# Latent attention: which engine rounds the weights and scales the first blocks' probabilities

## The chip, the cores and the metric

The program runs on one core of one Trainium2 chip. The metric is device time in microseconds (us). Three runs of the kernel before took 751.84, 752.97 and 751.84 us, median 751.84. One further execution was recorded by the hardware profiler; everything that is read from a profile or a trace below is from that one execution.

## The reference

One decoder block on 512 tokens of width 1024, float32. What matters here is the middle of it:

```python
xn = rmsnorm(x, norm_mix_g)
q_lat, kv_lat, k_rope, dq, dk, dv, gate_pre = split(xn @ w_in)
q  = rmsnorm(q_lat)  @ mla_w_uq      # 8 heads, 64 plain + 32 rotary columns each
kv = rmsnorm(kv_lat) @ mla_w_ukv     # 8 heads, 64 key + 64 value columns each
o_mla  = causal_attention([q_nope, rope(q_pe)], [k_nope, rope(k_rope)], v)   # softmax over 512 keys
o_diff = rmsnorm(attn(dq1, dk1, dv) - lam * attn(dq2, dk2, dv))              # 4 heads
x = x + (sigmoid(g1) * (o_mla @ w_branch_mla) + sigmoid(g2) * (o_diff @ w_branch_diff)) @ w_out
x = x + (silu(hn @ w_gate) * (hn @ w_up)) @ w_down
```

## The kernel before

**Products of three.** Every large matrix product is made of three matmuls. Each float32 operand is cut into a rounded high part and the rest, its low part, and `mm3` adds high x high (L301), high x low (L302) and low x high (L303) into one PSUM tile. For weights, `weights` loads a `raw` tile of up to 128x1024 (4 buffers), takes a `w` tile of twice that size (3 buffers), and calls `round_hi` (a copy that rounds: L264 on ScalarE or L266 on VectorE) and `round_lo` (raw minus high part: L269, on VectorE or GpSimd). The list `w_eng` says which engines do the two. The rest of the work that follows a product is the same everywhere: `split` writes a PSUM result as high part (ScalarE, L251 or L253) and low part (VectorE, L255 or L257).

**Stages.** At first the input is transposed and the latents are projected (to about 50 us in the trace). The middle stage holds both attentions and lasts to about 290 us: 8 heads of latent attention in 4 pairs, then 4 heads of differential attention. Then come the branch projections, the output projection and the feed-forward network, which is over half of the time and which the change does not touch.

**What sets the order in the middle stage.** A scheduler orders each engine's instructions by priority. The attention heads are written in `with urgent()`, so they go first whenever they are ready. Between them the scheduler places filling work, listed in `FILL`, `FILL_MLA` and `FILL_DIFF`: `mqk` (queries and keys of a pair of heads), `mv` and `v` (values), `pe` (rotary part of the queries), `mr` (DMAs that copy the rotated parts into the heads' tiles), `qk` (queries and keys of a differential head) and `gate` (gate projections). Each engine then runs its own instructions strictly in the order that the program holds.

**A head of latent attention** (`mla_head`) works through four blocks of queries, of 128, 256, 384 and 512 keys. For each, TensorE makes the scores (L633) in one of two `sc` tiles of PSUM. VectorE adds the mask and finds the maximum (L637), which also empties the `sc` tile. ScalarE takes the exponential with its sum (L156). VectorE inverts the sum (L640), and the block is multiplied by it: the first two blocks on GpSimd (L772, `P_POOL`), the other two on ScalarE (L774). Then TensorE transposes the blocks (L659) and multiplies them with the values (L781). A third block of scores cannot be written before the first one's tile has been emptied by L637.

**GpSimd's other work in the stage** stays: two of the four steps of the rotation of each differential projection (L566 and L567), part of the norm after each differential head (L698, L711), and the low parts of three weight tiles at the start of the stage (a gate and the first pair of latent heads), which are still under `W_ENG0`.

Of the kernel before, what the change touches and what calls it, by code (L numbers as in the profile page):

```python
# [17 lines left out]
ALU = mybir.AluOpType  # L18
# [25 lines left out]
W_POOL = "a0 a1 a4 b0 b1 b2 b3 b4 b5 b6 b7".split()  # L44
W_DVE = "b0 b1 b2 b3 b4 b5 b6 b7".split()
N_WARM = 8
P_POOL = (0, 1)
W_ENG0 = ['act', 'pool']
W_ENG = ['dve', 'pool']
W_ENG_DIFF = ['act', 'dve']  # L50
FILL = [[("gate", 0, 0)], [], [("pe", 0), ("mr", 0), ("gate", 0, 1), ("mv", 0)]]
FILL_MLA = [[("mqk", 1), ("mr", 1), ("v", 0), ("pe", 1)],
            [("mqk", 2), ("mr", 2), ("v", 1), ("mv", 1)],
# [40 lines left out]
def build(ctx, nc, tc, a, out):  # L94
# [12 lines left out]
    def PS(tag):  # L107
        return pp.tile([P, 512], F32, name=nm("ps_" + tag), tag=tag, bufs=PBUFS[tag])
# [151 lines left out]
    w_eng = list(W_ENG0)  # L260
# [219 lines left out]
    def gate(b, m):  # L480
        w = weights(kview("w_in", C_G + b * D + m * P, P), KD, P)
        ps = PS("mm")
        for k in range(KD):
            mm3(ps, [w[s][:, k, :] for s in range(2)], xa(k), k == 0, k == KD - 1)
        if m % 2 == 0:
            gate_tiles[b, m] = LF()
        gates[b, m] = gate_tiles[b, m - m % 2][:, (m % 2) * S:(m % 2 + 1) * S]
        nc.vector.tensor_mul(out=gates[b, m], in0=ps, in1=x_rms)
# [12 lines left out]
    def fill(work):  # L501
        for kind, *args in work:
            if kind == "gate":
                gate(*args)
            elif kind == "v":
                diff_v(*args)
            elif kind == "qk":
                qk[args[0]] = diff_qk(*args)
            elif kind == "pe":
                pe[args[0]] = mla_pe(*args)  # L510
            elif kind == "mv":
                mv[args[0]] = mla_v(*args)
            elif kind == "mqk":
                mqk[args[0]] = mla_qk(*args)
            elif kind == "mr":
                mla_rope(args[0], mqk[args[0]], pe[args[0] // 2])
# [66 lines left out]
    def diff_qk(h):  # L583


        u = diff_project(C_DQ + h * P)
        qs, k = [L_(), L_()], L_()
        for m, own, other in ((0, low, high), (1, high, low)):
            split(u[own], qs[0][own, m, :], qs[1][own, m, :], DIFF_SCALE)
            for q in qs:  # L590
                dma(r32(q[other, m, :]), r32(q[own, m, :]))
        u = diff_project(C_DK + h * P)
        for m, own, other in ((0, low, high), (1, high, low)):
            split(u[own], k[own, m, :], k[other, m, :])
        return [[(q[:, m, :], k[:, m, :]) for q in qs] for m in range(2)]
# [4 lines left out]
    def diff_v(c):  # L600
        w = [weights(kview("w_in", C_DV + c * 256, 256, k0, 4), 4, 256) for k0 in (0, 4)]
        for tp in range(2):
            ps = PS("mm")
            for t in range(2):
                for k in range(KD):
                    mm3(ps[:, t * 256:(t + 1) * 256], xa(k, slice((2 * tp + t) * P, (2 * tp + t + 1) * P)),
                        [w[k // 4][s][:, k % 4, :] for s in range(2)], k == 0, k == KD - 1)
            l = L_()
            for t in range(2):
                cs = slice(t * 256, (t + 1) * 256)  # L610
                split(ps[:, cs], l[:, 0, cs], l[:, 1, cs], x_rs[:, 2 * tp + t:2 * tp + t + 1])
            dv.append(l)


    def rope_key():
        pt = PS("tr")
        for t in range(NB):
            nc.tensor.transpose(out=pt[0:RD, t * P:(t + 1) * P], in_=latn[t][:, 640:672], identity=ident)
        kpe = L_()[0:RD]
        rope(pt[0:RD, :], kpe[:, 0, :], kpe[:, 1, :], cos_m, sin_m, shuf_m, 1.0, RD)  # L620
        return kpe
# [96 lines left out]
    def mla_pe(g):  # L718
        w = weights([a["mla_w_uq"][0][k * P:(k + 1) * P, :].rearrange("p (h d) -> p h d", d=96)
                     [:, 4 * g:4 * g + 4, 64:96] for k in range(3)], 3, P)  # L720
        ps = PS("mm")
        for k in range(3):
            mm3(ps, [w[s][:, k, :] for s in range(2)], [lat[k][:, s, :] for s in range(2)], k == 0, k == 2)
        pe = L_()
        rope(ps, pe[:, 0, :], pe[:, 1, :], cos_m, sin_m, shuf_m, MLA_SCALE)
        return pe
# [23 lines left out]
    def mla_v(g):  # L750
        w = weights(kview("mla_w_ukv", g * 512, 512), 2, 512, [(4, 64, 128)])
        v = []
        for tp in range(2):
            ps = PS("mm")
            for t in range(2):
                for k in range(2):
                    mm3(ps[:, t * 256:(t + 1) * 256],
                        [lat[3 + k][:, s, (2 * tp + t) * P:(2 * tp + t + 1) * P] for s in range(2)],
                        [w[s][:, k, :] for s in range(2)], k == 0, k == 1)
            l = T("L", [P, 2, 4, 2, 64], F32R)  # L760
            pv = ps.rearrange("p (t h d) -> p t h d", t=2, h=4)
            split(pv, l[:, :, :, 0, :], l[:, :, :, 1, :])
            v.append(l)
        return v

    def mla_head(qk, v, pair, o, h):
        q, k = qk[h]
        blocks = []
        for i, p in enumerate(prob_tiles()):
            r, = scores([([(q[0:96, a_, :], k[0:96, b_, :]) for a_, b_ in ((0, 0), (0, 1), (1, 0))], p)], i)  # L770
            if i in P_POOL:
                nc.gpsimd.tensor_scalar(out=p, in0=p, scalar1=r, scalar2=0.0, op0=ALU.mult, op1=ALU.add)  # L772
            else:
                nc.scalar.activation(out=p, in_=p, func=AF.Copy, scale=r)  # L774
            blocks.append(p)
        pt = transposed(blocks)
        c = 2 * (pair % 2) + h
        ps = PS("pv")
        for s in range(2):
            for j in range(NB):  # L780
                nc.tensor.matmul(out=ps[:, j * P:S], lhsT=v[j // 2][:, j % 2, c, :, :].rearrange("p s d -> p (s d)"),  # L781
                                 rhs=pt[:, s, OFF[j]:OFF[j] + S - j * P], start=s == 0 and j == 0,
                                 stop=s == 1 and j == NB - 1)
        u = tmp()[:64]
        nc.scalar.activation(out=u, in_=ps[64:P, :], func=AF.Copy)
        nc.vector.tensor_add(out=u, in0=ps[0:64, :], in1=u)
        rows = slice(64 * h, 64 * h + 64)
        split(u, o[rows, 0, :], o[rows, 1, :])
# [13 lines left out]
    mqk, pe, mv = {}, {}, {}  # L802
    fill([("mqk", 0)])
    kpe = rope_key()
    fill(FILL[2])
    o_mla = []
    for p in range(4):
        o = L_()
        o_mla.append(o)
        w_eng[:] = W_ENG  # L810
        fill(FILL_MLA[p])
        with urgent():
            for h in range(2):
                mla_head(mqk[p], mv[p // 2], p, o, h)


    o_diff, parts = [], []
    w_eng[:] = W_ENG_DIFF
    for h in range(4):
        fill(FILL_DIFF[h])  # L820
        with urgent():
# [179 lines left out]
```

## Time and profile before

| | |
|---|---|
| Three runs, us | 751.84, 752.97, 751.84 |
| The profiled execution's own time, us | 753.9 |
| Its span, us | 752.1 |
| TensorE busy | 737.0 us, 98% of the span |
| VectorE busy | 414.7 us, 55% |
| ScalarE busy | 326.8 us, 43% |
| GpSimd busy | 104.3 us, 14% |

Rows of the profile name the engines PE (TensorE matmuls), PEld (its weight loads), DVE (VectorE), ACT (ScalarE), POOL (GpSimd) and SP (SyncE, which issues the DMAs). L269 is line 269 of the kernel. In a group's row stand the shapes, how often it occurs, its busy time in us, the mean time of one in ns, and the idle time before it with what ended it. A timeline's row begins with its start and its length in us; idle time before it stands in brackets at the end. A matmul's length is modelled, and matmuls overlap in the pipe, so the pace is read from the distance of their starts. PEclk is the share of the TensorE clock that was granted.

### The profile page before, as it was taken

What the parts mean: (1) busy time and instruction counts of PE and PEld (TensorE: products, weight loads), DVE (VectorE), ACT (ScalarE), POOL (GpSimd) and SP (SyncE); (2) the same over time, 40 slices, a digit from 0 to 9 for tenths busy, and PEclk for the clock granted to TensorE, in tenths of its full rate; (3) what the DMA queues carried; (4) which work ended last, traced back from release to release, by engine and by line L of the source; (5) the groups of instructions that cost most, each with busy time, mean ns of one, the idle gap of its engine ahead of it and who ended that gap; (6) DMA issues with size and microseconds to landing.
All of it is one profiled execution on the core that took longest, in us unless ns stands there. A gap on an engine that the chain in (4) does not pass through costs nothing.

```text
span 752.1 us, 9652 instructions
## 1 busy us (share of the span) xinstructions
PE 737.0 (98%) x3639; PEld 623.0 (83%) x3639; DVE 414.7 (55%) x800; ACT 326.8 (43%) x609; POOL 104.3 (14%) x94
## 2 busy tenths in 40 slices
PE   7999999999999999999999999999999999999996
PEld 5988889888888888788898888888888888888885
DVE  6968688898998745595453323333333332122424
ACT  6564558587667535644233323232322223122314
POOL 3505252631341001000000000000000000000302
PEclk9999999999999999999999999999999999999999
DMA  8404333552433322248023333333323232322203
GB/s 300 124 1 117 106 87 96 135 126 69 110 87 87 107 85 85 84 140 278 2 85 108 89 97 99 98 99 87 109 85 111 85 112 85 109 88 92 106 0 113
DMA packets 99820, 76.74 MB, mean 102 GB/s; under 512 B 6303, under 2 KB 86973, under 8 KB 99773
## 3 DMA queue, kind: packets, MB, share of 16 engines
q1 hardware_dynamic: 99773, 76.12, 34.3%
q8 instruction: 29, 0.48, 0.3%
q14 instruction: 18, 0.15, 0.1%
HBM read 69.81 MB, written 2.10 MB: 96 GB/s over the span
## 4 chain that ended last, share of the span: by engine, by line
PE 81%; DVE 9%; ACT 5%; POOL 2%; issue 2%; DMA 1%; SPq 0%; DVEq 0%; ACTq 0%
PE ps_mm L301 22%; PE ps_mm L303 22%; PE ps_mm L302 22%; PE ps_sc L633 2%; PE ps_sc L301 1%; PE ps_sc L302 1%; PE ps_tr L301 1%; PE ps_tr L302 1%; PE ps_tr L303 1%; PE ps_sc L303 1%; POOL t L567 1%; PE ps_tr L659 1%; ACT L L495 1%; DVE w L269 1%; DVE X L355 1%
## 5 line engine op out<-in xcount | busy, mean ns | idle before, releaser
L302 PE MATMUL ps_mm<-X,w 128*128 128x512 f32 (+1 forms) x568 | 217.0, 382 | 0.0
L301 PE MATMUL ps_mm<-X,w 128*128 128x512 f32 (+1 forms) x568 | 216.9, 382 | 0.1
L303 PE MATMUL ps_mm<-X,w 128*128 128x512 f32 (+1 forms) x568 | 216.6, 382 | 0.0
L269 DVE TENSOR_TENSOR w<-raw,w 128x1024 fp32r<-128x1024 f32 x92 | 116.3, 1266 | 165.4 <-ACT w L264 165.2
L264 ACT ACTIVATE w<-raw 128x1024 fp32r<-128x1024 f32 (+1 forms) x98 | 101.1, 1036 | 181.2 <-issue 78.9
L303 PEld LDWEIGHTS ps_mm<-X,w 128*128 128x128 f32 x568 | 106.9, 188 | 19.9 <-POOL w L269 0.3
L301 PEld LDWEIGHTS ps_mm<-X,w 128*128 128x128 f32 x568 | 106.7, 188 | 19.9 <-DVE t L565 0.2
L302 PEld LDWEIGHTS ps_mm<-X,w 128*128 128x128 f32 x568 | 106.8, 188 | 19.7 <-DVE X L255 0.2
L936 POOL TENSOR_TENSOR L<-L,P 128x512 f32<-128x512 f32 (+1 forms) x9 | 11.6, 1299 | 439.0 <-ACT t L935 439.0
L909 ACT ACTIVATE t<-ps_mm 128x512 f32<-128x512 f32 x22 | 13.2, 598 | 80.9 <-PE ps_mm L303 80.9
L910 DVE TENSOR_TENSOR t<-t,ps_mm 128x512 f32<-128x512 f32 x22 | 15.1, 688 | 59.7 <-PE ps_mm L303 59.7
L156 ACT ACTIVATE P<-P,sm 128x128 f32<-128x128 f32 (+3 forms) x64 | 35.8, 560 | 27.4 <-DVE sm L637 27.0
L269 POOL TENSOR_TENSOR w<-raw,w 128x1024 fp32r<-128x1024 f32 (+3 forms) x22 | 37.3, 1701 | 57.5 <-PE ps_tr L472 25.8
L633 PE MATMUL ps_sc<-L,L 96*128 96x128 f32 (+7 forms) x160 | 36.5, 327 | 1.5 <-DVE sm L637 1.5
L302 PE MATMUL ps_mm<-w,L 128*128 128x512 f32 (+1 forms) x100 | 37.2, 372 | 0.0
L301 PE MATMUL ps_mm<-w,L 128*128 128x512 f32 (+1 forms) x100 | 37.2, 374 | 0.0
L303 PE MATMUL ps_mm<-w,L 128*128 128x512 f32 (+1 forms) x100 | 37.1, 373 | 0.0
L301 PE MATMUL ps_mm<-L,w 128*128 128x512 f32 x90 | 35.2, 393 | 0.5 <-ACT w L264 0.5
L302 PE MATMUL ps_mm<-L,w 128*128 128x512 f32 x90 | 35.5, 394 | 0.0
L303 PE MATMUL ps_mm<-L,w 128*128 128x512 f32 x90 | 35.2, 393 | 0.0
L251 ACT ACTIVATE L<-t 64x512 fp32r<-64x512 f32 (+2 forms) x47 | 29.1, 623 | 13.6 <-POOL t L567 6.2
L255 DVE TENSOR_TENSOR L<-t,L 128x512 fp32r<-128x512 f32 (+2 forms) x37 | 29.6, 801 | 4.8 <-ACT L L251 4.5
(265 smaller groups left out, 1231.9 us busy)
## 6 DMA issues: line engine op xcount, KB each, us to landing
raw<-w_in SPq DMA_DIRECT2D x28, 512.0 KB, 4.0
raw<-w_ffn_gate SPq DMA_DIRECT2D x22, 512.0 KB, 3.9
raw<-w_ffn_up SPq DMA_DIRECT2D x22, 512.0 KB, 3.9
raw<-w_ffn_down SPq DMA_DIRECT2D x22, 512.0 KB, 3.6
L<-L SPq DMA_DIRECT2D x32, 128.0 KB, 2.9
raw<-w_out SPq DMA_DIRECT2D x8, 512.0 KB, 3.7
L<-x SPq DMA_DIRECT2D x8, 256.0 KB, 6.1
raw<-w_branch_mla SPq DMA_DIRECT2D x4, 512.0 KB, 3.4
```

The source lines that it names most:

```text
L156: return nc.scalar.activation(**kw)
L251: nc.scalar.activation(out=hi, in_=src, func=AF.Copy, scale=scale)
L255: nc.vector.tensor_sub(out=lo, in0=src, in1=r32(hi))
L264: nc.scalar.activation(out=o, in_=i, func=AF.Copy)
L269: (nc.vector if w_eng[1] == 'dve' else nc.gpsimd).tensor_sub(out=o, in0=i, in1=r32(hi))
L301: nc.tensor.matmul(out=o, lhsT=lh, rhs=rh, start=start, stop=False)
L302: nc.tensor.matmul(out=o, lhsT=lh, rhs=rl, start=False, stop=False)
L303: return nc.tensor.matmul(out=o, lhsT=ll, rhs=rh, start=False, stop=stop)
L633: nc.tensor.matmul(out=ps[:, :n], lhsT=q[:, i * P:n], rhs=k[:, 0:n], start=j == 0, stop=j == last)
L909: last_silu = nc.scalar.activation(out=g, in_=gate_ps, func=AF.Silu)
L910: nc.vector.tensor_mul(out=g, in0=g, in1=ps)
L936: nc.gpsimd.tensor_mul(out=xs, in0=xs, in1=g)
```

## The change

The two low-level helpers stay as they are; only the engines that they use in the latent attention's part change.

- From the filling work that follows `rope_key()` on (`FILL[2]`) and through `FILL_MLA`, high parts of weights are made on ScalarE and low parts on VectorE. Before, `FILL[2]` had ScalarE and GpSimd, and `FILL_MLA` VectorE and GpSimd. The differential part had ScalarE and VectorE already and keeps them.
- The first two blocks' probabilities of each latent head are multiplied on VectorE, not on GpSimd.

```diff
-P_POOL = (0, 1)
+P_DVE = (0, 1)
 W_ENG0 = ['act', 'pool']
-W_ENG = ['dve', 'pool']
-W_ENG_DIFF = ['act', 'dve']
+W_ENG = ['act', 'dve']
@@ mla_head
-            if i in P_POOL:
-                nc.gpsimd.tensor_scalar(out=p, in0=p, scalar1=r, scalar2=0.0, op0=ALU.mult, op1=ALU.add)
+            if i in P_DVE:
+                nc.vector.tensor_scalar(out=p, in0=p, scalar1=r, scalar2=None, op0=ALU.mult)
             else:
                 nc.scalar.activation(out=p, in_=p, func=AF.Copy, scale=r)
@@ the middle stage
     kpe = rope_key()
+    w_eng[:] = W_ENG
     fill(FILL[2])
     o_mla = []
     for p in range(4):
         o = L_()
         o_mla.append(o)
-        w_eng[:] = W_ENG
         fill(FILL_MLA[p])
@@ the differential heads
-    w_eng[:] = W_ENG_DIFF
     for h in range(4):
```

Since the scheduler places everything anew, the order changes on all engines in the middle stage: on TensorE from the first head's scores to the last differential head, on VectorE and ScalarE from the first weight tile of `FILL[2]`. Behind the last differential head it is the same as before. Lines of the changed kernel have numbers that are one or two lower.

The first place is VectorE at the first head's first block of scores. `w_134` and `w_136` are the two weight tiles of the values `v` of the differential heads, `w_142` is the weight tile of the second rotary projection, and `ps_sc_148`, `ps_sc_152` and `ps_sc_157` are the first three blocks of scores. Before:

```order
L266 CAST w_134_912<-raw_133_910 128x1024
L255 TENSOR_TENSOR L_121_863<-ps_mm_120_850,L_121_863 128x8x64
L266 CAST w_136_917<-raw_135_915 128x1024
L257 SCALAR_TENSOR_TENSOR L_123_867<-ps_mm_129_876,L_123_867 64x512
L266 CAST w_142_1032<-raw_141_1028 128x384
L637 ISA P_147_1054,sm_149_1059<-ps_sc_148_1055,mask_103 128x128
```

And in the changed kernel:

```order
L254 TENSOR_TENSOR L_121_863<-ps_mm_120_850,L_121_863 128x8x64
L268 TENSOR_TENSOR w_134_912<-raw_133_910,w_134_912 128x1024
L256 SCALAR_TENSOR_TENSOR L_123_867<-ps_mm_129_876,L_123_867 64x512
L268 TENSOR_TENSOR w_136_917<-raw_135_915,w_136_917 128x1024
L636 ISA P_147_1054,sm_149_1059<-ps_sc_148_1055,mask_103 128x128
L636 ISA sm_149_1059 128x1
L268 TENSOR_TENSOR w_142_1032<-raw_141_1028,w_142_1032 128x384
```

The three roundings to high parts are gone from VectorE, two low parts stand in their place, and the weight tile `w_142` now comes behind the first block's maximum, not ahead of it.

The second place is TensorE around the third block of scores, `ps_sc_157`. Before, it stands 13 matmuls behind the second block, and then the second tile of values, `ps_mm_139`, is begun:

```order
L303 MATMUL ps_mm_137_920<-w_134_912,X_1_62 128x256
L301 MATMUL ps_mm_137_920<-w_136_917,X_2_63 128x256
L633 MATMUL ps_sc_157_1078<-L_95_717,L_93_715 128x384 x3
L301 MATMUL ps_mm_139_974<-w_134_912,X_1_62 128x256
L302 MATMUL ps_mm_139_974<-w_134_912,X_1_62 128x256
```

In the changed kernel it stands 31 matmuls behind the second block, and the first tile of values goes on:

```order
L300 MATMUL ps_mm_137_920<-w_134_912,X_1_62 128x256
L301 MATMUL ps_mm_137_920<-w_134_912,X_1_62 128x256
L632 MATMUL ps_sc_157_1078<-L_95_717,L_93_715 128x384 x3
L302 MATMUL ps_mm_137_920<-w_134_912,X_1_62 128x256
L300 MATMUL ps_mm_137_920<-w_134_912,X_1_62 128x256
```

What moved is how much filling work TensorE has between the second and the third block of scores: 18 matmuls of 128x256 more.

## The prediction

> **What bounds the kernel now.** I read the page's first part, then the stretches of the middle stage, then who waited for whom on TensorE, then the timeline around the one long wait. The page says that TensorE bounds the whole:
>
> ```profile
> span 752.1 us, 9652 instructions
> PE 737.0 (98%) x3639; PEld 623.0 (83%) x3639; DVE 414.7 (55%) x800; ACT 326.8 (43%) x609; POOL 104.3 (14%) x94
> ```
>
> The stage that the change touches, cut into stretches (columns: PE, PEld, DVE, ACT and POOL busy us, granted clock, DMA):
>
> ```profile
> 55.00:75.00 20.00, 20.00 (x109) 16.71 (x107) 16.73 (x28) 9.45 (x15) 9.42 (x6) 1.00 0.45 110
> 75.00:250.00 175.00, 173.16 (x983) 151.62 (x982) 150.75 (x365) 117.25 (x259) 60.77 (x50) 0.99 0.39 100
> ```
>
> TensorE is idle for 175.00 - 173.16 = 1.84 us there. VectorE is the second busiest, 150.75 of 175 us (86%). All that TensorE waited for between 75 and 330 us:
>
> ```profile
> PE ps_sc L633 <- DVE sm L637: 1.5, 1, 1.5
> PE ps_mm L301 <- ACT w L264: 0.5, 1, 0.5
> PE ps_pv L781 <- DVE PT L255: 0.3, 1, 0.3
> ```
>
> So the change cannot win much by relieving an engine on average: it can win the 1.5 and the 0.3 us that are waits for VectorE in this stage, and what hangs on them. The 0.5 us is at the branch projections, where no order changes. The long wait, in the timeline:
>
> ```profile
> 74.94 0.85 PE L633 MATMUL ps_sc<-L,L 96*128 96x128 f32 x6
> 75.63 0.28 PE L301 MATMUL ps_mm<-w,X 128*128 128x256 f32 x1
> 75.90 2.43 POOL L269 TENSOR_TENSOR w<-raw,w 128x1024 fp32r<-128x1024 f32 x1 [0.63 <-DVE w L266]
> 76.34 2.20 DVE L266 CAST w<-raw 128x384 fp32r<-128x384 f32 x1
> 76.70 0.28 PE L301 MATMUL ps_mm<-w,X 128*128 128x256 f32 x1
> 76.82 0.28 PE L302 MATMUL ps_mm<-w,X 128*128 128x256 f32 x1
> 77.06 0.28 PE L301 MATMUL ps_mm<-w,X 128*128 128x256 f32 x1
> 78.47 0.27 DVE L637 CUSTOM_DVE_ANT_0 P<-ps_sc,mask 128x128 f32<-128x128 f32 x1
> 78.80 0.79 PE L633 MATMUL ps_sc<-L,L 96*128 96x384 f32 x3 [1.47 <-DVE sm L637]
> 81.01 0.41 PE L301 MATMUL ps_mm<-w,X 128*128 128x256 f32 x1
> 81.22 0.41 PE L302 MATMUL ps_mm<-w,X 128*128 128x256 f32 x1
> ```
>
> TensorE stops at 77.34 and waits 1.47 us, because the third block of scores needs the tile that the first block's maximum (L637) empties. That stands on VectorE behind a rounding (L266) of 384 columns that took 2.20 us. Another of the same form, 11 us earlier in the timeline, took 0.34:
>
> ```profile
> 65.02 0.34 DVE L266 CAST w<-raw 128x384 fp32r<-128x384 f32 x1
> ```
>
>  While it ran, GpSimd worked on a low part from 75.90 to 78.33, and the rounding ended 0.21 us later: VectorE was held up by GpSimd. Then TensorE runs at half speed for a while. Its matmuls of 256 columns start 0.12 us apart at 76.70 and 0.21 us apart at 81.01. By stretches (same columns):
>
> ```profile
> 76.30:79.60 3.30, 1.82 (x12) 1.31 (x11) 3.24 (x6) 1.68 (x4) 3.00 (x2) 1.00 0.73 185
> 79.70:83.00 3.30, 3.30 (x16) 3.30 (x17) 2.23 (x9) 1.80 (x5) 0.85 (x2) 0.50 0.91 265
> 83.10:86.50 3.40, 3.40 (x29) 3.27 (x28) 1.14 (x6) 1.67 (x4) 0.00 (x0) 1.00 0.10 35
> ```
>
> The granted clock was 0.50 from 79.7 to 83.1 us, right behind the stretch in which TensorE was busy for only 1.82 of 3.30 us, and 1.00 on both sides. I take the wait as its cause. At 0.21 us a matmul instead of 0.12, 3.4 us do the work of 3.4 x 0.12 / 0.21 = 1.94, so this cost 1.46 us.
>
> **The change part by part.** Rows for the prices (the same forms by group):
>
> ```profile
> L567 POOL TENSOR_TENSOR t<-t,t 128x512 f32<-128x512 f32 x8 | 14.2, 1782 | 0.2
> L772 POOL TENSOR_SCALAR P<-P,sm 128x256 f32<-128x256 f32 x8 | 3.8, 479 | 6.8 <-DVE sm L640 6.7
> L772 POOL TENSOR_SCALAR P<-P,sm 128x128 f32<-128x128 f32 x8 | 3.0, 374 | 14.9 <-DVE sm L640 14.9
> L266 DVE CAST w<-raw 128x1024 fp32r<-128x1024 f32 x8 | 7.8, 976 | 0.4 <-issue 0.4
> L266 DVE CAST w<-raw 128x384 fp32r<-128x384 f32 x4 | 3.2, 810 | 0.3 <-PE ps_mm L303 0.3
> L266 DVE CAST w<-raw 128x512 fp32r<-128x512 f32 x1 | 2.6, 2569 | 0.0
> L266 DVE CAST w<-raw 128x256 fp32r<-128x256 f32 x3 | 0.9, 300 | 0.8 <-PE ps_mm L303 0.8
> L269 DVE TENSOR_TENSOR w<-raw,w 128x1024 fp32r<-128x1024 f32 x92 | 116.3, 1266 | 165.4 <-ACT w L264 165.2
> L255 DVE TENSOR_TENSOR PT<-ps_tr,PT 128x384 fp32r<-128x384 f32 x24 | 13.1, 549 | 2.0 <-ACT PT L251 1.9
> L255 DVE TENSOR_TENSOR PT<-ps_tr,PT 128x512 fp32r<-128x512 f32 x12 | 8.2, 683 | 0.3 <-ACT PT L251 0.3
> L255 DVE TENSOR_TENSOR L<-t,L 64x512 fp32r<-64x512 f32 x16 | 15.2, 953 | 1.7 <-ACT L L251 1.4
> L255 DVE TENSOR_TENSOR L<-ps_mm,L 64x512 fp32r<-64x512 f32 x8 | 5.5, 686 | 0.5 <-ACT L L251 0.3
> L460 DVE TENSOR_SCALAR L<-L,sm 128x256 f32<-128x256 f32 x4 | 1.1, 349 | 0.0
> L264 ACT ACTIVATE w<-raw 128x1024 fp32r<-128x1024 f32 x27 | 28.2, 1053 | 22.4 <-PE ps_mm L303 22.4
> L264 ACT ACTIVATE w<-raw 128x384 fp32r<-128x384 f32 x1 | 0.5, 523 | 1.2 <-PE ps_mm L303 1.2
> ```
>
> *GpSimd* loses 19 low parts (9 of 1024 columns, 5 of 384, 3 of 256, 2 of 512) and the 16 products, 3.8 + 3.0 us. It waited most of the time before, so its own time is worth nothing; what counts is that it no longer holds VectorE. The loads of weights get their `raw` tile back from VectorE instead; the rows of waits show TensorE waiting for no load, so I put nothing.
>
> *VectorE* loses the 16 roundings: 7.8 + 3.2 + 2.6 + 0.9 = 14.5 us. It gains the 19 low parts: 9 x 1.27 = 11.4; 5 x 0.55 = 2.7; 2 of 512 at 0.68 (the same form in L255) = 1.4; 3 of 256, which no row shows: between 0.35 (a one-input form of 256) and 0.55 (the two-input form of 384), taken at 0.41 by the slope between 384 and 512 columns, so 1.2. The products cost 8 x 0.35 for 256 columns (L460 is the same operation); for 128 the bounds are 0 and 0.35, taken at 0.27 by GpSimd's own ratio of 374 to 479: together 5.0 us. In sum 16.7 + 5.0 = 21.7 us come and 14.5 go. L255 from a tile in SBUF takes 953 ns where the same form from PSUM takes 686; most of 16 x 0.27 = 4.3 us of that is GpSimd's low parts in its way, and goes too. Net 21.7 - 14.5 - 4.3 = +2.9 us on 16.73 + 150.75 = 167.5 busy of 195 us between 55 and 250. That makes 87%: VectorE does not become the bound, but it has no more air than before. These 2.9 us are off TensorE's path as long as filling matmuls are queued in front of it; without that cover they would all show.
>
> *ScalarE* gains the 16 high parts: 8 x 1.05 + 4 x 0.52, and by the slope between the two rows 0.63 for 512 columns and 3 x 0.42 for 256: 12.4 us on 117.25 of 175, 74%, hidden by the same matmuls. A low part on VectorE now waits for ScalarE's high part, and behind it in VectorE's queue stand the maxima that TensorE waits for: 0 to 1.05 us each time, nothing where the scheduler leaves room.
>
> *The long wait goes.* In the new order VectorE runs, from the end of the tile L_121 on, two low parts of 1024 columns, one 64x512 step and then the first maximum. Before, L_121 ended at 73.4:
>
> ```profile
> 72.71 0.69 DVE L255 TENSOR_TENSOR L<-ps_mm,L 128x512 fp32r<-128x512 f32 x1
> ```
>
> So the tile is empty at 73.4 + 2 x 1.27 + 0.69 + 0.28 = 76.9 us if L_121 is not later than before. Ahead of it VectorE gets 0.55 + 1.27 + 0.68 + 0.55 + 0.41 = 3.5 us of low parts and loses 1.3 us of roundings; of these 2.2 us the 3.27 idle us between 55 and 75 (16.73 of 20 busy) take all or nothing, so 76.9 to 79.1. I take 77.6, a third of the way, as most of the gaps lie early. TensorE comes to the third block 31 matmuls behind 75.63, at 75.63 + 31 x 0.12 = 79.35: ahead of the tile's release in no case. The wait of 1.47 us goes, and with it the stretch at half clock, 1.46 us. The 0.29 us at 111.93 (the third row of the waits) is a wait for VectorE among GpSimd's low parts, so I count it as gone too; that it stays is the other bound.
>
> *What is late next.* The two weight tiles of values: the first low part is ready 1.27 us behind L_121, at 74.7 to 76.9, and needed at 75.75; the second at 76.6 to 78.8, needed at the 13th matmul, 75.63 + 12 x 0.12 = 77.1. Both are late by 0 to 1.7 us at most, 0.3 at my value. The first scores (74.94) need rotated parts by DMA:
>
> ```profile
> 70.14 3.25 SPq L126 DMA_DIRECT2D L<-L  x5
> L<-L SPq DMA_DIRECT2D x8, 128.0 KB, 2.3
> ```
>
> The third of the five is the last that they need: issued by 72.1 and landed 2.3 us later, at 74.4. Its source comes from VectorE 0 to 1 us later now: a wait of 0 to 0.5 us. Behind that, each head's first two products stand on VectorE, and whatever is queued behind them (the next maximum, and so TensorE's next block of scores) waits 0.3 us longer; ahead of TensorE stand 13 or more filling matmuls in most places, 1.6 to 3 us, which hide it. For all this I put 1.0 us, between 0 and one wait as long as the old one with its half-clock stretch, 2.9.
>
> *Sum*, against the profiled execution's own 753.9 us (its span of 752.1 and 1.8 around it): 753.9 - 1.5 - 1.5 - 0.3 + 1.0 = 751.6. The median of the three runs lies 2.1 us below that execution, so 749.5 for the median of the new one.
>
> A rule that speaks against the change: the rotation's steps stay on GpSimd, 8 of 1.78 us (L567) among them, and VectorE gets more low parts and the products beside them. At two meetings of half a length VectorE loses 1.8 us, and TensorE nothing while its queue holds. The Trainium skill, "SBUF — State Buffer", Who interferes with whom, says why: one port pair is shared by VectorE and GpSimd, a VectorE step with two SBUF inputs or in a two-port mode and a GpSimd step exclude each other for the whole instruction. The trace agrees: 2.20 us instead of 0.34, ending with GpSimd.
>
> **The rivals.**
>
> *The half-clock stretch stays, or was not in the three runs.* It may have another cause than the wait, or the timed runs may have gone without it, which could be part of their 2.1 us. Then only 1.5 + 0.3 are won: 751.84 - 1.8 + 1.0 = 751.0, within 0.2% of before. For it: the runs differ by 1.1 us among themselves. Against: it follows the emptiest stretch at once. The Trainium skill, "TensorE: Matmul & The Clock Gate", What's actually happening, speaks for this rival: it has the clock halved after an idle window of about 3.4 us. The trace shows 0.50 behind a wait of 1.47 us.
>
> *VectorE gives it back.* At 87% with an order kept strictly, several short waits of 0.3 to 0.5 us arise where low parts of 1.27 us stand ahead of a maximum. Six of them make 2.4 us more than I counted: 751.9, no change.
>
> *Slower.* A low part of 1.27 us stands ahead of a maximum or of a transposed block, and TensorE has too few filling matmuls: it waits over 1.4 us and gets a half-clock stretch on top, 2.9 us each. One such place cancels the gain; from the second on the kernel is slower: 749.5 + 2 x 2.9 = 755.3; with one place and the short waits, 749.5 + 2.9 + 1.0 = 753.4. For it: VectorE is at 150.75 of 175 us. Against: 86% left waits of 1.8 us in all so far.
>
> *The change does nothing that it says.* Excluded by the order: the low parts stand on VectorE.
>
> **How the numbers follow.** A measurement of this kernel tells some 0.2% from no change, 1.5 us: below 750.3 is faster, above 753.3 slower. My forecast, 749.5, gets 0.5; its own range is 748.5 (no new wait) to 750.3. The half-clock rival gets 0.2 and the short waits 0.13, both no change; slower 0.17. The range must leave out no more than 2 in 10: from 748.0 (748.5 less half of the 1.1 us by which the runs differ) to 753.4 it takes in the first three cases and the near edge of the last.
>
> **What would show it.** Right: no wait of TensorE over 0.5 us between 70 and 90 us, granted clock 1.00 there, roundings to high parts gone from VectorE, the low parts of 1024 columns at about 1.25 us, and TensorE at the branch projections some 2 to 3 us earlier. Wrong: a wait for VectorE of over 1 us in the rows of waits, a stretch at 0.50 anywhere between 50 and 740 us, or the first scores waiting for a DMA.

## The result and the profile after

The changed kernel took 756.12 us (median of eight executions, 754.52 to 759.15) against 751.86 for the kernel before on the same chip: a ratio of 1.006, 95% interval 1.0041 to 1.008. It is slower by 4.3 us, where 749.5 was predicted with a range of 748.0 to 753.4. One of the eight executions of the kernel before took 816.58 us and is left out of the ratio. The execution that was profiled took 755.07 us. TensorE still bounds it, and no engine has become a new bound (from the first part of the page):

```profile
span 753.1 us, 9630 instructions
PE 735.8 (98%) x3639; PEld 620.4 (82%) x3639; DVE 415.5 (55%) x819; ACT 335.9 (45%) x625; POOL 64.8 (9%) x59
```

VectorE has 0.8 us more than before, ScalarE 9 us more, GpSimd 40 us less. The old place near 77 us is mended: in the stretches of the changed kernel TensorE is busy throughout and the granted clock is 1.00, where the kernel before had 1.82 of 3.30 and then 0.50.

```profile
76.30:79.60 3.30, 3.30 (x30) 3.30 (x29) 3.18 (x11) 1.68 (x6) 0.00 (x0) 1.00 0.97 216
79.70:83.00 3.30, 3.30 (x27) 3.21 (x26) 1.04 (x5) 1.04 (x3) 0.00 (x0) 1.00 0.80 272
```

But four other waits have come. All that TensorE waited for between 50 and 330 us:

```profile
PE ps_tr L704 <- DVE L L696: 1.7, 1, 1.7
PE ps_sc L632 <- DMA L<-L: 0.9, 1, 0.9
PE ps_pv L780 <- ACT PT L250: 0.9, 1, 0.9
PE ps_mm L300 <- DVE t L564: 0.9, 1, 0.9
PE ps_mm L300 <- ACT w L263: 0.5, 1, 0.5
```

The last one was there before. The other four make 4.4 us, against 1.5 + 0.3 us that went. Pieces of the middle stage show where (columns: length, then PE, PEld, DVE, ACT, POOL busy, granted clock, DMA; rows left out are marked):

```profile
50.00:75.00 25.00, 24.65 (x131) 20.16 (x129) 21.71 (x42) 13.89 (x23) 0.00 (x0) 1.00 0.35 90
75.00:100.00 25.00, 24.45 (x172) 22.93 (x173) 18.69 (x57) 16.52 (x40) 0.00 (x0) 1.00 0.40 110
...
175.00:200.00 25.00, 23.19 (x116) 19.04 (x115) 21.73 (x54) 15.96 (x35) 5.67 (x4) 1.00 0.29 71
...
250.00:290.00 40.00, 38.31 (x183) 31.82 (x181) 22.81 (x46) 17.29 (x31) 3.54 (x3) 1.00 0.30 92
```

In the kernel before (here from its second profile, e9) TensorE was busy throughout in the last two of them:

```profile
175.00:200.00 25.00, 25.00 (x124) 21.07 (x123) 22.74 (x55) 18.13 (x38) 6.54 (x4) 1.00 0.33 85
...
250.00:290.00 40.00, 40.00 (x189) 33.25 (x188) 22.63 (x36) 15.82 (x25) 4.87 (x3) 1.00 0.30 93
```

In the changed kernel TensorE loses 1.81 us between 175 and 200 and 1.69 us between 250 and 290. From 200 us on, the work belongs to the differential attention, whose engines the change does not touch. The two largest places, in the timeline. First the end of the last latent head:

```profile
182.15 0.39 PE L302 MATMUL ps_mm<-X,w 128*128 128x512 f32 x1
182.37 0.51 PE L632 MATMUL ps_sc<-L,L 128*128 128x384 f32 x2
182.57 1.06 ACT L263 ACTIVATE w<-raw 128x1024 fp32r<-128x1024 f32 x1 [0.65 <-PE ps_mm L302]
...
183.66 1.23 DVE L268 TENSOR_TENSOR w<-raw,w 128x1024 fp32r<-128x1024 f32 x1 [0.46 <-ACT w L263]
...
184.53 0.47 ACT L250 ACTIVATE PT<-ps_tr 128x384 fp32r<-128x384 f32 x1
...
185.05 0.92 PE L780 MATMUL ps_pv<-PT,L 128*128 128x256 f32 x4 [0.86 <-ACT PT L250]
...
188.31 0.50 PE L300 MATMUL ps_mm<-X,w 128*128 128x512 f32 x1 [0.85 <-DVE t L564]
```

No filling matmul (`ps_mm`) stands between 182.15 and 188.31 us. Whatever is late there, a high part on ScalarE or a low part on VectorE, TensorE has nothing to do meanwhile. The second place:

```profile
260.37 1.23 DVE L268 TENSOR_TENSOR w<-raw,w 128x1024 fp32r<-128x1024 f32 x1 [0.33 <-ACT w L263]
...
260.54 0.45 PE L632 MATMUL ps_sc<-L,L 128*128 128x512 f32 x1
...
262.12 0.42 DVE L696 CAST L<-t 128x512 fp32r<-128x512 f32 x1
...
262.69 0.47 PE L704 MATMUL ps_tr<-L,ones_r 128*128 128x512 f32 x1 [1.69 <-DVE L L696]
```

Here the norm's matmul with ones (L704) comes directly behind the last scores, with no filling matmul between.

The order of TensorE's program says the same. Counted between the scores into tile 449 and those into tile 500 (the end of the last latent head and the start of the first differential one), the kernel before has 19 filling matmuls and the changed one none; ahead of the third differential head's L704 it is 22 and none (the first two heads have none or one there in both, and no long wait, so the count marks a place where cover is missing and not yet a wait). A piece of the program after and before (number, line, tiles; rows left out are marked):

```
after
973 L632 MATMUL ps_sc_449_2287<-L_290_1659,L_288_1657 128x384
974 L632 MATMUL ps_sc_449_2287<-L_290_1659,L_289_1658 128x384
975 L780 MATMUL ps_pv_408_2106<-PT_404_2086,L_219_1396 128x512
...
979 L658 MATMUL ps_tr_467_2331<-ident_98,P_427_2239 128x128
980 L632 MATMUL ps_sc_458_2309<-L_290_1659,L_288_1657 128x512
981 L632 MATMUL ps_sc_458_2309<-L_290_1659,L_289_1658 128x512
982 L780 MATMUL ps_pv_408_2106<-PT_404_2086,L_221_1412 128x256
before
951 L659 MATMUL ps_tr_467_2331<-ident_98,P_427_2239 128x128
952 L302 MATMUL ps_mm_420_2172<-X_2_63,w_419_2169 128x512
953 L303 MATMUL ps_mm_420_2172<-X_2_63,w_419_2169 128x512
...
958 L302 MATMUL ps_mm_425_2212<-X_1_62,w_424_2209 128x512
959 L633 MATMUL ps_sc_458_2309<-L_290_1659,L_288_1657 128x512
```

So the question for the experiments: is it the engines' load (weights' parts of 1.05 and 1.23 us in the way), the 16 products on VectorE, or the sequence into which the scheduler puts TensorE's work once the engines differ?

### The profile page after: what moved, and what is told of

The parts are those of the page before. It is cut to its first block, busy times and chain, and to the rows that moved or that the text cites. A ratio compares the mean times of both kernels' runs of the same rounds, so it can differ in the third digit from the quotient of the medians.

```text
span 753.1 us, 9630 instructions
## 1 busy us (share of the span) xinstructions
PE 735.8 (98%) x3639; PEld 620.4 (82%) x3639; DVE 415.5 (55%) x819; ACT 335.9 (45%) x625; POOL 64.8 (9%) x59
## 4 chain that ended last, share of the span: by engine, by line
PE 78%; DVE 12%; ACT 5%; DMA 2%; issue 2%; SPq 1%; POOL 0%; DVEq 0%; ACTq 0%; POOLq 0%
PE ps_mm L302 21%; PE ps_mm L301 21%; PE ps_mm L300 21%; PE ps_sc L632 2%; DVE w L268 2%; DVE P L636 1%; PE ps_sc L300 1%; PE ps_sc L301 1%; PE ps_tr L301 1%; PE ps_tr L300 1%; PE ps_tr L302 1%; PE ps_sc L302 1%; PE ps_tr L658 1%; PE ps_pv L780 1%; ACT L L494 1%
## 5 line engine op out<-in xcount | busy, mean ns | idle before, releaser
L268 DVE TENSOR_TENSOR w<-raw,w 128x1024 fp32r<-128x1024 f32 (+3 forms) x111 | 131.6, 1188 | 169.1 <-ACT w L263 168.7
L300 PE MATMUL ps_mm<-X,w 128*128 128x512 f32 (+1 forms) x568 | 217.0, 383 | 1.0 <-DVE t L564 0.9
L263 ACT ACTIVATE w<-raw 128x1024 fp32r<-128x1024 f32 (+2 forms) x114 | 113.2, 999 | 182.2 <-issue 78.9
L300 PEld LDWEIGHTS ps_mm<-X,w 128*128 128x128 f32 x568 | 106.7, 188 | 21.0 <-DVE t L564 1.0
L300 PE MATMUL ps_mm<-w,L 128*128 128x512 f32 (+1 forms) x100 | 37.1, 373 | 0.0
L300 PE MATMUL ps_mm<-L,w 128*128 128x512 f32 x90 | 35.3, 394 | 0.5 <-ACT w L263 0.5
L636 DVE CUSTOM_DVE_ANT_0 P<-ps_sc,mask 128x128 f32<-128x128 f32 (+3 forms) x64 | 30.6, 478 | 4.5 <-PE ps_sc L632 3.9
L632 PEld LDWEIGHTS ps_sc<-L,L 96*128 96x128 f32 (+1 forms) x160 | 26.6, 189 | 4.5 <-DMA L<-L 1.2
```

What stands on the lines that cost most here:

```text
L263: nc.scalar.activation(out=o, in_=i, func=AF.Copy)
L268: (nc.vector if w_eng[1] == 'dve' else nc.gpsimd).tensor_sub(out=o, in0=i, in1=r32(hi))
L300: nc.tensor.matmul(out=o, lhsT=lh, rhs=rh, start=start, stop=False)
L632: nc.tensor.matmul(out=ps[:, :n], lhsT=q[:, i * P:n], rhs=k[:, 0:n], start=j == 0, stop=j == last)
L636: nc.vector.tensor_tensor_reduce(out=m, in0=ps[:, :n], in1=mask[:, S - n:], scale=-1.0, scalar=3.4e38, op0=ALU.add, op1=ALU.min, accum_out ...
```

## Experiments

All ratios are to the kernel before on the same chip, with 95% intervals. The kernel before took 751.80 to 751.88 us (medians) in these comparisons. A ratio weighs all runs and lies nearer to the quotient of their means than to that of the medians.

**e1: the weights' part alone.** In the changed kernel the products go back to GpSimd.

```diff
-P_DVE = (0, 1)
+P_POOL = (0, 1)
...
-            if i in P_DVE:
-                nc.vector.tensor_scalar(out=p, in0=p, scalar1=r, scalar2=None, op0=ALU.mult)
+            if i in P_POOL:
+                nc.gpsimd.tensor_scalar(out=p, in0=p, scalar1=r, scalar2=0.0, op0=ALU.mult, op1=ALU.add)
```

> Only the weights' part of the change: high parts on ScalarE and low parts on VectorE, the first blocks' products stay on GpSimd. Theory of the load (the weights' parts of 1.05 and 1.23 us stand in ScalarE's and VectorE's queues ahead of steps that TensorE waits for): 755 to 757 us, as with the whole change, with waits of TensorE of over 0.8 us near 184, 187 and 261 us. Theory of the products (the 16 products on VectorE are what delays the maxima): 751 to 752 us. Theory of the order (the scheduler gives TensorE another sequence, in which filling matmuls are missing at some places, and the engines are not to blame): it says nothing sure, since the sequence moves again; 750 to 757 us, with the waits at other places than in the whole change.

Measured: 755.96 us, ratio 1.0051 (1.0032 to 1.0071), with the waits at L704 (2.0 us), L300 (0.9 us) and one of 2.5 us for the rotated parts. As slow as the whole change; the products are not needed for the loss. Time and waits are about what the theory of the load said. But TensorE's program lacks the filling matmuls at the same two places as in the changed kernel, so this run cannot tell load from order.

**e2: the products alone.** The kernel before with L772 on VectorE.

```diff
-P_POOL = (0, 1)
+P_DVE = (0, 1)
...
-                nc.gpsimd.tensor_scalar(out=p, in0=p, scalar1=r, scalar2=0.0, op0=ALU.mult, op1=ALU.add)
+                nc.vector.tensor_scalar(out=p, in0=p, scalar1=r, scalar2=None, op0=ALU.mult)
```

> Only the products of the first two blocks go from GpSimd to VectorE; the weights' parts stay as before. Theory of the load: 751.5 to 752.5 us, with the wait of 1.5 us behind the held rounding near 77 us still there. Theory of the products: 754 us or more. Theory of the order: 750 to 757 us, by where the scheduler then has filling matmuls.

Measured: 754.98 us, ratio 1.0034 (1.0022 to 1.0047). The old wait of 1.5 us stays, and two of 0.6 us come, for a maximum near 176 us and behind the rotation (L565) near 191 us, although the 19 filling matmuls between tiles 449 and 500 are all there. Either half of the change is slow by itself, so neither e1 nor e2 singles out a cause. The next runs hold TensorE's sequence fixed.

**e3 and e4: engines and sequence crossed.** At the end of the program every matmul is tied behind the one that precedes it in the other kernel's sequence (issue order only, no wait for its end). The table holds 3638 matmuls as runs of neighbours. The other engines' sequences are what the scheduler then makes around it.

```diff
+def keep_order(tc, nc, engine, table):
+    seen = [i for i in nc.cur_bb.bb.instructions if i.engine == engine and type(i).__name__ not in NOT_KEPT]
+    order = []
+    for r in table.split():
+        first, n = (r + "+1").split("+")[:2]
+        order += range(int(first), int(first) + int(n))
...
+    for x, y in zip(order, order[1:]):
+        tc.add_manual_dep(seen[y], seen[x].name, mybir.DependencyInfo(mybir.DependencyClass.NoSync, mybir.DependencyReason.DATA),
+                          reason="keep_order")
...
         build(ctx, nc, tc, a, out)
+        keep_order(tc, nc, mybir.EngineType.PE, ORDER_PE)
```

> The whole change, but TensorE runs its matmuls in exactly the sequence of the kernel before; the other engines' sequences are the scheduler's. Theory of the load: 754 to 757 us, since the same weights' parts are on the same engines. Theory of the order: 750.0 to 752.0 us, without the waits at 184, 187 and 261 us, and without the old one at 77 us.

> The engines of the kernel before, but TensorE runs its matmuls in exactly the sequence of the changed kernel. Theory of the load: 752 us or less. Theory of the order: 753.5 to 757 us, with waits of TensorE near 187 and 261 us as in the changed kernel.

Measured: e4, the old engines in the new sequence, took 758.55 us, ratio 1.0086 (1.0073 to 1.0099), the slowest of all, with these waits among others:

```profile
PE ps_tr L705 <- DVE L L697: 1.7, 1, 1.7
...
PE ps_pv L781 <- ACT PT L251: 0.9, 1, 0.9
PE ps_mm L301 <- DVE t L565: 0.9, 1, 0.9
```

They are the three late waits of the changed kernel, each of the same length and behind the same step, with the engines of before (at 265.6, 187.9 and 191.2 us). They belong to TensorE's sequence. That e4 is 1.5 us above its range fits further waits that the changed kernel does not have (1.0 us for a low part of GpSimd, 2.1 us for maxima); the profiled execution, 759.38 us, also has a stretch at half clock behind the first of the three. e3, the new engines in the old sequence, has none of the three. Its time, 754.37 us, ratio 1.0031 (1.0019 to 1.0043), is in the range of the theory of the load, but its waits are not those: what it pays for is another one, which neither theory had.

```profile
PE ps_sc L632 <- DMA L<-L: 3.1, 2, 2.3
```

What SyncE issued ahead of it, and how long the transfers took (KB each, median us from issue to landing):

```profile
103.95 1.97 SPq L125 DMA_DIRECT2D raw<-w_in  x2
105.96 2.95 SPq L125 DMA_DIRECT2D L<-L  x4
```

```profile
raw<-w_in SPq DMA_DIRECT2D x2, 512.0 KB, 5.9
L<-L SPq DMA_DIRECT2D x4, 128.0 KB, 5.8
```

Two weight loads went ahead of the copies of the rotated parts. In the kernel before the copies went first (109.14, the loads at 112.08). A stretch at half clock follows the wait, by the windows of e3:

```profile
111.00:113.70 2.70, 0.40 (x5) 0.23 (x3) 2.61 (x7) 1.41 (x4) 0.00 (x0) 1.00 0.32 67
114.90:118.40 3.50, 3.50 (x18) 3.40 (x16) 2.02 (x9) 2.56 (x8) 0.00 (x0) 0.51 0.00 0
```

**e5: both sequences old.** As e3, and SyncE's DMAs too stand in the old sequence. VectorE's and ScalarE's sequences are still the scheduler's own.

```diff
         keep_order(tc, nc, mybir.EngineType.PE, ORDER_PE)
+        keep_order(tc, nc, mybir.EngineType.SP, ORDER_SP)
```

> The whole change, with TensorE's matmuls and SyncE's DMAs both in exactly the sequences of the kernel before. Run e3 had TensorE's old sequence, but two weight loads of 512 KB went ahead of the copies of the rotated parts and the copies landed 5.8 us after their issue instead of 2.3. Theory of the order (TensorE's and the DMA queue's sequence decide): 749.5 to 751.5 us, no wait of TensorE for a DMA over 0.5 us near 74 and 111 us, none for VectorE over 0.5 us. Theory of the load (VectorE and ScalarE deliver later whatever the order): 754 us or more, with the waits for the rotated parts still there.

Measured: 750.41 us (750.18 to 751.54), ratio 0.9977 (0.9967 to 0.9987): faster than before. The copies land after 2.3 us again:

```profile
105.29 2.42 SPq L125 DMA_DIRECT2D L<-L  x4
107.75 1.40 SPq L125 DMA_DIRECT2D raw<-w_in  x2
```

Apart from a wait of 0.6 us for the first rotated parts nothing is left between 50 and 300 us. The same engines that lose 4.3 us in the scheduler's own sequences gain 1.4 us with the old ones of TensorE and SyncE.

**e7: one load moved.** The changed kernel with every engine in its own sequence, and one DMA moved in SyncE's table. Piece of the table: 44 is the load, 28, 27 and 29 are the copies; the first line is the changed kernel's own sequence in the same numbers.

```diff
-... 39+5 44 28 27 29 30 35 ...
+... 39+5 28 27 29 44 30 35 ...
```

> The changed kernel with all engines in its own sequences, and one DMA moved: the load of 288 KB of mla_w_uq that stands ahead of the copies of the rotated parts at 70 us is issued behind the first three of them. Theory of the order: the wait of 1.0 us of the first scores near 74.4 us goes; 753.5 to 755.5 us, 1 us below the changed kernel. Theory of the load: the rotated parts come late from VectorE, and the wait stays over 0.5 us; 755 to 757 us.

Measured: 754.69 us, ratio 1.0037 (1.0023 to 1.005), 1.4 us below the changed kernel. The wait of the first scores shrank from 0.9 to 0.5 us and did not go:

```profile
PE ps_sc L632 <- DMA L<-L: 0.5, 1, 0.5
```

The load in front accounts for about half of that wait in the profile; for the other half the rotated part comes later from VectorE, as e5 (0.6 us with the copies in front) and e12 below (none without the first list's low parts on VectorE) bear out. Both theories had a share here. The 1.4 us of the medians are more than the 0.4 us of the profiles, and what makes up the rest is not shown.

**e8: the old wait by itself.** The kernel before in its own sequences, with one step of VectorE moved. Piece of VectorE's table: 162 is the rounding of 384 columns, 168 the first block's maximum; the first line is the sequence of before in the same numbers.

```diff
-... 157 151 162 168 152 ...
+... 157 151 168 162 152 ...
```

> The kernel before with all engines in its own sequences, and one step of VectorE moved: the first block's maximum ahead of the rounding of 384 columns that GpSimd holds up for 2.2 us. What the old wait is worth by itself: if the timed runs have the stretch at half clock behind it, as the profiled one had, 1.5 + 1.5 less: 748.9 us; if they went without it, 1.5 less: 750.4 us; if the wait only moves on to the next maximum, 751.9 us.

Measured: 751.48 us, ratio 0.9989 (0.9981 to 0.9998), close to the third case. The maximum now comes at once, but the rounding behind it is held up all the same, and the step after that is the next that TensorE waits for:

```profile
75.23 2.38 POOL L269 TENSOR_TENSOR w<-raw,w 128x1024 fp32r<-128x1024 f32 x1 [0.63 <-DVE w L266]
...
75.88 1.96 DVE L266 CAST w<-raw 128x384 fp32r<-128x384 f32 x1
...
77.87 0.69 DVE L257 SCALAR_TENSOR_TENSOR L<-ps_mm,L 64x512 fp32r<-64x512 f32 x1
...
78.71 0.35 PE L301 MATMUL ps_mm<-w,X 128*128 128x256 f32 x1 [1.53 <-DVE L L257]
```

What costs is the time that VectorE is held, 1.6 us on top of the rounding's own 0.34; which waiting step pays for it is a matter of order.

**e9: the kernel before once more**, for a second profile.

> The kernel before once more, for a second profile of it. If the timed runs of 751.9 us went without the stretch at half clock at 79.7 to 83.1 us: a profiled execution near 751.9 us shows the granted clock at 1.00 there and the wait of 1.5 us still in place. If the stretch belongs to the wait: 0.50 there in this execution too, and what is missing to 753.9 us lies at the start.

Measured: 752.22 us, ratio 1.0001 (0.9991 to 1.001). The profiled execution took 752.58 us, and its windows show the wait without the half clock:

```profile
76.30:79.60 3.30, 1.83 (x14) 1.53 (x12) 3.27 (x5) 1.68 (x4) 3.01 (x2) 1.00 0.74 187
79.70:83.00 3.30, 3.27 (x24) 3.07 (x24) 2.41 (x8) 1.62 (x5) 1.00 (x3) 1.00 0.95 248
```

The same 1.5 us of idling brings the stretch at 0.50 in one execution and not in another. The timed runs of the kernel before beside e14 to e16, which have no trace, fit that: 14 of 21 took 751.3 to 752.0 us at a granted clock of 0.997 or 0.998 over the run, the other 7 took 752.9 to 753.4, all but one at 0.996 or less.

**e10 to e13: the parts with the old sequences.** TensorE and SyncE stand in the old sequences, as in e5, and the engines differ. e10 has the engines of e1, e11 those of e2; e12 is the change without the first list, e13 the kernel before with the pairs' high parts on ScalarE.

```diff
e12, in the changed kernel
-    w_eng[:] = W_ENG
     fill(FILL[2])
+    w_eng[:] = W_ENG
e13, in the kernel before
-W_ENG = ['dve', 'pool']
+W_ENG = ['act', 'pool']
```

> Only the weights' part of the change (products stay on GpSimd), with TensorE's and SyncE's sequences of the kernel before, as in e5. If the weights' part carries the gain of e5: 750.4 us, without the old wait of 1.5 us near 77 us. If the products carry it: 751.9 us.

> Only the products' part of the change, with TensorE's and SyncE's sequences of the kernel before. If the products cost nothing by themselves and the 3 us of e2 came from the order: 751.9 us, with the old wait of 1.5 us still there. If the products are a cost of their own (each stands ahead of the next maximum): 753 us or more. If they are the gain of e5: 750.4 us.

> The whole change except for the first list of filling work, whose weights keep ScalarE and GpSimd; old sequences as in e5. If the 0.8 us that TensorE still waits in e5 for the rotated parts near 74 us comes from the low parts on VectorE ahead of the rotation: that wait goes, 749.6 us. If GpSimd's low parts there hold VectorE up again (as they did with the rounding): 751 us or more, with a step of VectorE of over 2 us between 70 and 79 us.

> Kernel before with one letter of the change: the pairs' high parts on ScalarE instead of VectorE, the low parts and the products stay on GpSimd; old sequences. It tells which half of the weights' part gains: if it is that VectorE is rid of the roundings, 750.4 us; if it is that GpSimd no longer holds VectorE up, 751.9 us or more, with a step of VectorE of twice its usual length ending with a low part of GpSimd near 77 us.

Measured: e10 750.27 us, ratio 0.9973 (0.9964 to 0.9983); e11 753.29 us, 1.0018 (1.001 to 1.0027); e12 749.83 us, 0.9968 (0.9956 to 0.998); e13 751.74 us, 0.9997 (0.9989 to 1.0006). The weights' part carries the whole gain. The products alone cost 1.5 us, half of what e2 lost: the old wait stays, and a second one of 0.85 us comes at 116 us, where VectorE works without a gap from 114.5 us on, and one of 0.3 us at 212 us:

```profile
PE ps_sc L633 <- DVE sm L637: 2.3, 2, 1.5
```

Beside the weights' part they cost nothing that can be told (e5 against e10, 750.41 and 750.27). In e12 the wait for the rotated parts is gone (0.6 us in e5's rows). e13 shows that ridding VectorE of the roundings is not enough: the old wait goes, but GpSimd's low parts hold up other steps, not near 77 us as expected but from 97 us on. A step of the rotation on VectorE (L566), 0.68 us long in e14, took 2.85 beside a low part of GpSimd. The maximum behind it came late, ScalarE waited 2.04 us for that and then worked without a gap up to the transposed block for which TensorE waited 0.81 us:

```profile
96.95 2.39 POOL L269 TENSOR_TENSOR w<-raw,w 128x1024 fp32r<-128x1024 f32 x1 [2.37 <-ACT w L264]
97.04 2.85 DVE L566 TENSOR_TENSOR t<-t,tab 128x512 f32<-128x512 f32 x1
...
99.81 0.68 DVE L637 CUSTOM_DVE_ANT_0 P<-ps_sc,mask 128x512 f32<-128x512 f32 x1
...
100.53 0.72 ACT L156 ACTIVATE P<-P,sm 128x512 f32<-128x512 f32 x1 [2.04 <-DVE sm L637]
...
105.77 0.91 PE L781 MATMUL ps_pv<-PT,L 128*128 128x256 f32 x4 [0.81 <-ACT PT L251]
```

**e14 to e16: the version that this points to, and what the scheduler makes of it.** e14 is the kernel before with one line changed and the old sequences kept; e15 is the same without the tables; e16 has the engines of e12 without the tables.

```diff
-W_ENG = ['dve', 'pool']
+W_ENG = ['act', 'dve']
...
+        keep_order(tc, nc, mybir.EngineType.PE, ORDER_PE)
+        keep_order(tc, nc, mybir.EngineType.SP, ORDER_SP)
```

> The version that the runs so far point to: only the pairs' lists of filling work get ScalarE and VectorE, the first list keeps ScalarE and GpSimd, the products stay on GpSimd; TensorE's and SyncE's sequences as before. e12 has 749.83 us with the products on VectorE; e5 against e10 says that the products are worth 0.1 us there: 749.3 to 749.9 us. If products on VectorE cost 1.4 us wherever they stand, as e11 has it: 748.4 us.

> The same engines as e14, with the sequences that the scheduler itself then makes. Theory of the order: slower than e14 by 3 us or more, 753 to 757 us, with waits of TensorE over 0.8 us in the stretch from 180 to 265 us or for the rotated parts. If it was the first list or the products that made the scheduler's sequence bad: 750 us.

> The same engines as e12 (the whole change except for the first list), with the sequences that the scheduler itself then makes. Theory of the order: slower than e12 by 3 us or more, 753 to 757 us, the waits near 187 and 261 us among them. If the first list's low parts on VectorE were what moved the sequence for the worse: 750 us.

Measured: e14 749.58 us (749.21 to 749.72), ratio 0.9966 (0.9953 to 0.9978), the fastest of all. e15 753.12 us (751.32 to 754.7), 1.0008 (0.9998 to 1.0019); e16 753.57 us (751.63 to 756.38), 1.0022 (1.0009 to 1.0035). TensorE's waits between 50 and 330 us, e14:

```profile
PE ps_mm L301 <- ACT w L264: 0.5, 1, 0.5
PE ps_mm L301 <- DVE L L257: 0.3, 1, 0.3
```

and e15:

```profile
PE ps_mm L301 <- DVE t L565: 0.8, 1, 0.8
PE ps_sc L633 <- DVE sm L637: 0.8, 2, 0.6
PE ps_mm L301 <- ACT w L264: 0.5, 1, 0.5
```

e15's waits lie at 184 to 188 us, and its program too has no filling matmul between tile 449 and tile 500. So the gap there comes with any of these edits of the weights (e1's program has it as well). The wait at 261 us, expected in e16, is in neither: only the sequences that the scheduler makes with the first list changed bring it (the changed kernel's, which e4 and e7 keep, and e1's). Each pair, in medians:

| engines | scheduler's own sequences | old sequences |
|---|---|---|
| the whole change | 756.12 | 750.41 (e5) |
| weights (e1, e10) | 755.96 | 750.27 |
| products (e2, e11) | 754.98 | 753.29 |
| the change without the first list (e16, e12) | 753.57 | 749.83 |
| the pairs' weights alone (e15, e14) | 753.12 | 749.58 |

Part of each difference of medians may lie in how often a wait brings a stretch at half clock. Between the fastest runs of each pair the differences are 4.3, 4.0, 0.8, 2.2 and 2.1 us.

## Why the prediction was wrong

*The step that failed* is "What is late next". The prediction took the covers from the order before: "ahead of TensorE stand 13 or more filling matmuls in most places, 1.6 to 3 us, which hide it", and put 1.0 us in all for what is late. In the new order there are none at the two places that matter. The profile after has 4.4 us of new waits in its rows, and the three late ones (3.5 us) come back one for one with the old engines in the new sequence (e4) and vanish with the new engines in the old one (e3, e5). Two of its signs of being wrong came, a wait for VectorE of over 1 us (1.7) and the first scores waiting for a DMA (0.9). The prediction read the new order near 77 us, at the wait that it expected to go, and not at the ends of the heads, where filling work runs out.

*The loads of weights*, "I put nothing": this failed as well. In the sequence that the scheduler makes for SyncE with these engines, loads of weights stand ahead of copies that TensorE waits for; that `raw` tiles come free earlier once VectorE makes the low parts is a likely reason and was not tried. In e3 it made 2.3 us of waiting and a stretch at half clock; in the changed kernel it is a part of the 0.9 us at 74 us, of which moving one load took away 0.4 in the profile (e7). The 0 to 0.5 us that the prediction gave to the first scores were too little by as much.

*The half-clock stretch*, -1.5 us: this was the first rival, and for the stretch it is what happened. e9 shows the wait with the clock at 1.00; two in three of the timed runs of the kernel before, by time and clock, seem to have gone without the stretch. The 2.1 us between the profiled execution and the median, which the sum carried along as a constant, were for the larger part that very stretch (753.9 with it, 752.58 without it in e9), so the sum took it off twice. The first profile has another stretch at 0.50, from 11.4 to 14.8 us, which the prediction passed over; by the third block of scores (78.80 us, 79.03 in e9) that execution was no later than e9.

*The long wait goes*, -1.5 us: right. With the sequences held, the weights' part gains 751.80 - 750.27 = 1.53 us (e10). That GpSimd holding VectorE was the cause is borne out twice: e8 moves the maximum ahead and the wait moves on to the next step, and e13 leaves the low parts on GpSimd and finds another step held up, with a wait of TensorE at the end of its chain.

*The engines' sums* were nearly right. VectorE was to get 5.0 us for the products, and e11 has 419.8 busy us against 414.8 in e9. It was to lose 2.1 us net by the weights, and e10 has 412.4, 2.4 less. ScalarE was to get 12.4 and got 338.0 - 327.0 = 11.0 in e10. Products and weights together, +2.9 us on VectorE, came to +1.6 in e5 and +0.8 in the changed kernel. None of these sums decided the time.

*The slower rival* had the right picture, low parts and too few filling matmuls, with a chance of 0.17 and 755.3 us for two places. But it had VectorE's load as its cause, and e4 has the old engines and is slower still. It also counted a stretch at half clock behind each wait; the profiled execution has none in the middle stage, and four waits in place of two. That its sum comes near 755.07 us is luck. What the load does depends on the cover: in e14 and e15 the same engines lie 3.5 us apart.

*What stays open*: why the scheduler spends its filling work earlier with these engines was not tried, and VectorE's and ScalarE's sequences were not exchanged by themselves. Of the changed kernel's 4.3 us the profiled execution shows 3.2 (755.07 against 751.86), and the waits explain 2.6 of these (4.4 - 1.8). The rest of the 4.3 fits the runs of 756 to 759 us at clocks of 0.993 to 0.996, beside 0.998 in the profiled one, but those runs have no trace, and the fastest run of all, 754.52 us, has 0.995.

## What to carry to other kernels

Where a scheduler decides the order, an edit of engines is two changes: price both, by counting the filling work ahead of each place where the bounding engine waits for another, in the new order. When a sound edit comes out slower, run it once in the old order, and the unedited kernel once in the new one; here that separated a gain of 1.4 us from a loss of 5.7. And look at which loads then stand in the DMA queue ahead of copies that the bounding engine waits for.

## What the runs showed of the hardware

A stretch at half clock seems to be worth 1.5 to 1.7 us a time and comes in some executions of one program and not in others: e15's runs fall into 751.3 to 751.7 us at a granted clock of 0.997 to 0.998, 753.1 to 753.3 at 0.995, and 754.6 to 754.7 at 0.994. Its profiled execution is of the last kind and has two stretches on end:

```profile
183.50:186.90 3.40, 2.56 (x13) 1.50 (x11) 3.06 (x11) 2.26 (x6) 0.00 (x0) 1.00 0.52 133
187.00:190.40 3.40, 2.75 (x7) 2.17 (x8) 3.40 (x7) 0.41 (x2) 3.23 (x3) 0.50 0.05 13
190.40:193.70 3.30, 3.30 (x9) 2.62 (x8) 3.14 (x10) 2.90 (x7) 2.07 (x2) 0.50 0.02 5
```

The clock halves behind a stretch in which TensorE was still busy for 2.56 of 3.40 us by the rows, whose ends are modelled. In every trace the changes of the clock lie on a grid of 3.41 us, which begins elsewhere in each execution. Cut along it, the old wait left TensorE busy for 1.93 us of one piece (76.24 to 79.66) in the first profile of the kernel before, and the clock halved; in e9 it left 2.04 us (75.52 to 78.93), and the clock stayed. Busy time alone does not decide it: at the start of e9 a piece with 1.71 us (7.25 to 10.66) was followed by full clock. The Trainium skill, "TensorE: Matmul & The Clock Gate", What's actually happening, has the activity judged in free-running windows of 3.4 us, which agrees with the grid and with the length (3.41 us in the kernel before). The same section has the half clock come after at least one idle window; that a whole window must be idle does not agree with these rows.

Copies of 128 KB landed 5.8 us after issue instead of 2.3 with two loads of 512 KB issued just ahead (e3, e5). The Trainium skill, "DMA: Bandwidth & Descriptors", Two DMAs through the same engine are not ordered, says that within one queue of one DMA engine descriptors start in order; the trace agrees, as the small copies paid for the bytes in front of them.
